# A scaled matmul on one core: the rows of two output tiles leave in transfers of 6, 5, 105 and 12 rows

## The chip, the cores and the metric

The kernel runs on one core of a Trainium2 chip. The core has a matrix engine (TensorE, PE in the profile), three engines for elementwise work (VectorE = DVE, ScalarE = ACT, GpSimd = POOL), an engine that here only issues transfers (SyncE = SP), and sixteen DMA engines that move data between the chip's memory (DRAM, "HBM" in the profile) and the on-chip memory of 128 partitions. The metric is the device time of one execution in microseconds (us), as a median over several runs.

## The reference

```python
"x": np.random.randn(16, 512, 1024).astype(np.float32)
"weight": np.random.randn(1024, 768).astype(np.float32)
"scale": np.float32(0.1)
"add_value": np.random.randn(16, 512, 768).astype(np.float32)

return (scale * np.matmul(x, weight) + add_value).astype(np.float32)
```

Seen as matrices, `x` is 8192 x 1024, `add_value` and the output are 8192 x 768. Every element of the three is moved once, and the weight once.

## The kernel before

The 8192 rows are 64 tiles of 128 rows, one row to a partition. They form three blocks of 24, 24 and 16 tiles. Within a block of g tiles, partition p holds g neighbouring rows of the matrix, so that several neighbouring tiles of a partition are one stretch of bytes in DRAM: a tile's row of output is 3 KB, and twelve neighbouring tiles are one run of 36 KB in each partition.

The buffers are rings: `xs` has 16 slots for tiles of `x`, `ao` has 32 slots for tiles of `add_value`, in which the output is also made (tile t is in slot (t + 8) mod 32, and the weight uses the first eight slots at the start).

What each engine does, in the order of one tile's way:
- **SyncE** (`sync_engine`) issues every transfer, in the order of the string `STREAM`, and waits ahead of each until its slots are free or its results made. A word such as `x16+8` loads tiles 16 to 23 of `x`, `a` loads `add_value`, `w` the weight, and `o32+16` stores the output tiles 32 to 47. All are 128 rows. The stores take turns on four semaphores (`o_sem`); a store also waits for the one that used its semaphore four stores earlier.
- **ScalarE and GpSimd** (`mover`) share the cast of `x` to bf16: a move is four tiles, and each engine casts half of the pieces, eight instructions for each move, into one of two buffers `va`. A move waits for the load (`x_sem`) and for the buffer to be free (`turned`). The first four moves are written out, the other twelve are in a loop of three turns.
- **VectorE** (`vector_engine`) transposes two tiles at a time from `va` into `xt` (`turn`, line 190; it waits for both movers), and finishes two tiles at a time (`finish`, line 199): product x scale + add_value, from `mm` into `ao`. Each finish adds 2 to the semaphore `made`, which starts at `MADE`.
- **TensorE** (`tensor_engine`, lines 222 and 248) multiplies the tiles in order, eight pieces of the contraction for each, in two parts of 512 and 256 columns.

The last store (`o62+2`) is issued behind the section with the hand-written order. The other stores of the second half are `o32+16`, `o48+8` and `o56+6`. The order of the transfers on SyncE is written out by hand; so are all waits.

The change touches `transfer` (line 97), `sync_engine` (line 107) and `mover` (line 151).

Of the kernel before, what the change touches and what calls it, by code (L numbers as in the profile page):

```python
# [7 lines left out]
P = 128  # L8
BLOCKS = ((0, 24), (24, 24), (48, 16))
G = 8  # L10
X_SLOTS = 16
# [5 lines left out]
MOVE = 4  # L17
O_LANES = 4
HALVED = (0, 1)
FETCH = 128  # L20

STREAM = """
    x0+4 w0+8 x4+8 a0+8 x12+4 a8+8 x16+8 a16+8 x24+8 a24+8 x32+8 o0+8 o8+8 a32+8 x40+8
    a40+8 x48+8 x56+4 o16+8 o24+8 a48+4 x60+4 a52+4 a56+8 o32+16 o48+8 o56+6 o62+2
"""


# [7 lines left out]
def kernel(  # L35
# [17 lines left out]
    T = M // P  # L53
# [4 lines left out]
    def blocks(flat):  # L58
        return [(s, g, flat[P * s:P * (s + g), :].rearrange("(p t) n -> p t n", t=g))
                for s, g in BLOCKS]  # L60

    x_v, add_v, out_v = blocks(x_f), blocks(add_f), blocks(out_f)
    w_v = weight.rearrange("(p r) n -> p r n", p=P)

    def rows(view, s, n):
        for first, g, block in view:
            if first <= s and s + n <= first + g:
                return block[:, s - first:s - first + n, :]
        raise ValueError((s, n))
# [5 lines left out]
    ao = const.tile([P, A_SLOTS, N], fp32, name="ao")  # L75
# [10 lines left out]
    by_act, by_pool, pool_go, turned, casts, done, made = (  # L86
        tc.alloc_semaphore(name)
        for name in ("by_act", "by_pool", "pool_go", "turned", "casts", "done", "made"))
    TURNED = MOVE * VA_BUFS
    MADE = TURNED + MM_BUFS  # L90

    def slots(t, n):
        k = (t + G) % A_SLOTS
        assert k + n <= A_SLOTS
        return slice(k, k + n)

    def transfer(eng, op, s, n):
        if op == "w":
            return eng.dma_start(ao[:, s:s + n, :], w_v[:, s:s + n, :])  # L99
        if op == "x":  # L100
            k = s % X_SLOTS
            return eng.dma_start(xs[:, k:k + n, :], rows(x_v, s, n))  # L102
        if op == "a":
            return eng.dma_start(ao[:, slots(s, n), :], rows(add_v, s, n))
        return eng.dma_start(rows(out_v, s, n), ao[:, slots(s, n), :])

    def sync_engine(eng):
        loads, stores, known = [], [], {}

        def need(sem, value):  # L110
            if known.get(id(sem), 0) < value:
                eng.wait_ge(sem, value)
                known[id(sem)] = value

        for op, s, n in stream[:-1]:
            last = s + n
            if op == "w":
                sem = w_sem
            elif op == "x":
                lane = s % X_SLOTS // MOVE  # L120
                if last > X_SLOTS:
                    moved = 8 * (last - X_SLOTS) // MOVE
                    need(by_act, moved)
                    need(by_pool, moved)
                if n == 2 * MOVE:
                    eng.sem_inc(x_sem[lane + 1], 16)
                sem = x_sem[lane]
            elif op == "a":
                if loads:
                    need(a_sem, 16 * len(loads))  # L130
                if slots(s, n).start < KJ:
                    need(casts, KJ)
                if s >= A_SLOTS:
                    for i, (a, b) in enumerate(stores):
                        if a < last - A_SLOTS and s - A_SLOTS < a + b:
                            need(o_sem[i % O_LANES], 16 * (i // O_LANES + 1))
                if s % G:
                    sem = a_late
                else:
                    sem = a_sem  # L140
                    loads.append((s, n))
            else:
                i = len(stores)
                if i >= O_LANES:
                    need(o_sem[i % O_LANES], 16 * (i // O_LANES))
                need(made, MADE + last)
                sem = o_sem[i % O_LANES]
                stores.append((s, n))
            transfer(eng, op, s, n).then_inc(sem, 16)

    def mover(eng, copy, parity, count, go=None):
        if go is None:
            eng.preload_act_table(mybir.ActivationFunctionType.Copy)  # L153

        def move(q, step, landed, freed):
            eng.wait_ge(x_sem[q], landed)
            if freed is not None:
                eng.wait_ge(turned, freed)
            if go is not None:
                eng.sem_inc(go, 1)  # L160
            k = MOVE * q
            src = xs[:, k:k + MOVE, :].rearrange("p i (b k) -> p i b k", b=4)
            for t in range(0, MOVE, step):
                for a in (parity, parity + 2):
                    for b in range(4):
                        copied = copy(va[q % VA_BUFS][32 * b:32 * b + 32, t:t + step, a, :],  # L166
                                      src[32 * a:32 * a + 32, t:t + step, b, :])
                        if step == MOVE or b % 2:
                            copied.then_inc(count, 1)

        for q in range(X_SLOTS // MOVE):
            move(q, MOVE // 2 if q in HALVED else MOVE, 16,
                 MOVE * (q + 1) if q >= VA_BUFS else None)
        with eng.Fori(32, T + 1, X_SLOTS) as i:
            for q in range(X_SLOTS // MOVE):
                move(q, MOVE, i, i + (4 * q - 12) if q < 3 else i)

    def vector_engine(eng):
        ao_g = ao.rearrange("p (g t) n -> p g t n", t=G)
# [73 lines left out]
    for eng in (nc.scalar, nc.gpsimd):  # L253
        eng.addr_align(FETCH, offset=0, max_nops=0)
    with tc.tile_critical(no_gpsimd_drain=True):  # L255
        sync_engine(nc.sync)
        mover(nc.scalar, nc.scalar.copy, 0, by_act)
        mover(nc.gpsimd, nc.gpsimd.tensor_copy, 1, by_pool, pool_go)
        vector_engine(nc.vector)
        tensor_engine(nc.tensor)  # L260
    transfer(nc.sync, *stream[-1])


# [33 lines left out]
```

## Time and profile before

| | |
|---|---|
| median of 3 runs | 209.46 us (209.31 to 209.88) |
| the profiled execution | 209.42 us |
| its span, first to last instruction | 207.6 us |
| bytes read from and written to DRAM | 61.87 MB and 25.17 MB |
| mean rate over the span | 419 GB/s |
| TensorE busy | 82% |
| GpSimd busy | 67% |
| ScalarE busy | 66% |
| VectorE busy | 59% |
| packets of SyncE's queue, share of 16 DMA engines' span | 98.0% |

The page of the profile gives busy times, the span in 40 slices, the DMA queues, the chain of work that ended last, groups of instructions and the transfers' times from issue to landing. Other views of the same execution list the instructions in order of time, who waited for whom, and busy times in chosen windows. A transfer issued is not a transfer done: SyncE's issue instruction is short, and the data move later. A packet in the DMA rows is one run of bytes or one write that reports completion.

### The profile page before, as it was taken

The numbers are of one execution on the slowest core, as the hardware profiler recorded it, in microseconds if no ns is written. First come the engines' busy times: TensorE is split into PE (matmuls) and PEld (weight loads), VectorE is DVE, ScalarE is ACT, GpSimd is POOL, SyncE is SP. The second block draws the span as 40 slices with busy tenths as digits, with TensorE's granted clock in tenths as the row PEclk, the third lists the DMA queues.
The fourth block names the chain that finished last, engine by engine and source line by source line (L and its number), as shares of the span: only waits on it lengthen the run. The fifth ranks groups of instructions, "written<-read, shape, count | busy, mean of one in ns | idle before, by whom it ended". The sixth has DMA issues, their size and how long they took to land.

```text
span 207.6 us, 2250 instructions
## 1 busy us (share of the span) xinstructions
PE 170.7 (82%) x1024; PEld 50.8 (24%) x512; DVE 123.0 (59%) x66; ACT 137.8 (66%) x145; POOL 138.3 (67%) x148
## 2 busy tenths in 40 slices
PE   0001993699999999999999999999999899999800
PEld 0000230123223333333333333333333233333200
DVE  0038304937677767776777677767774867777320
ACT  2494199999596969696969079999696959100000
POOL 0399299999797969696969179999796959200000
PEclk9999999699999999999999999999999999999995
DMA  6999999999999999899999999999999999998994
GB/s 224 458 432 410 448 455 404 455 455 404 404 473 436 420 388 505 350 421 440 436 431 447 404 450 459 404 420 436 436 421 428 412 455 469 455 445 355 434 420 173
DMA packets 4034, 87.05 MB, mean 419 GB/s; under 512 B 448, under 2 KB 448, under 8 KB 576
## 3 DMA queue, kind: packets, MB, share of 16 engines
q1 hardware_dynamic: 4032, 87.03, 98.0%
q14 instruction: 2, 0.02, 0.0%
HBM read 61.87 MB, written 25.17 MB: 419 GB/s over the span
## 4 chain that ended last, share of the span: by engine, by line
PE 59%; DMA 26%; POOL 5%; DVE 4%; issue 2%; SPq 0%; DVEq 0%; POOLq 0%
PE mm L248 39%; PE mm L222 20%; DMA xs<-in_x_dram 11%; DMA out_dram<-ao 10%; DMA ao<-in_add_value_dram 5%; POOL va L166 5%; DVE xt L190 2%; DVE ao L199 2%; SPq L99 0%; SPq L102 0%; DVEq L199 0%; DVEq L196 0%; POOLq L160 0%; DVEq L188 0%; SPq L292 0%
## 5 line engine op out<-in xcount | busy, mean ns | idle before, releaser
L248 PE MATMUL mm<-w_bf,xt 128*128 128x512 bf16 x512 | 170.3, 385 | 26.0 <-DVE w_bf L183 20.2
L166 POOL CAST va<-xs 32x1024 bf16<-32x1024 f32 (+1 forms) x144 | 138.1, 959 | 39.1 <-DMA xs<-in_x_dram 18.6
L166 ACT CAST va<-xs 32x1024 bf16<-32x1024 f32 (+1 forms) x144 | 136.5, 948 | 38.4 <-DMA xs<-in_x_dram 20.5
L222 PE MATMUL mm<-w_bf,xt 128*128 128x256 bf16 x512 | 141.4, 276 | 0.0
L199 DVE SCALAR_TENSOR_TENSOR ao<-mm,ao 128x1536 f32 (+1 forms) x32 | 56.2, 1755 | 58.7 <-PE mm L222 46.2
L248 PEld LDWEIGHTS mm<-w_bf,xt 128*128 128x128 bf16 x512 | 50.8, 99 | 145.4 <-issue 138.4
L190 DVE STREAM_TRANSPOSE xt<-va 128x1024 f32<-128x1024 f32 x32 | 65.2, 2037 | 16.9 <-POOL va L166 16.9
L183 DVE CAST w_bf<-ao 128x3072 bf16<-128x3072 f32 x2 | 4.3, 2170 | 0.0
L153 ACT ACT_TABLE_LOAD x1 | 1.3, 1283 | 1.3 <-SPq L255 1.3
L278 POOL MEMSET const-float32-0.0<- 128x1 f32 x1 | 0.1, 98 | 0.2 <-issue 0.2
L278 POOL MEMSET const-bfloat16-1.0<- 128x1 bf16 x1 | 0.1, 100 | 0.0
L278 POOL MEMSET const-uint8-127<- 128x1 uint8 x1 | 0.1, 98 | 0.0
L278 POOL MEMSET const-float32-1.0<- 128x1 f32 x1 | 0.1, 97 | 0.0
## 6 DMA issues: line engine op xcount, KB each, us to landing
xs<-in_x_dram SPq DMA_DIRECT2D x6, 4096.0 KB, 20.5
ao<-in_add_value_dram SPq DMA_DIRECT2D x7, 3072.0 KB, 17.0
out_dram<-ao SPq DMA_DIRECT2D x5, 3072.0 KB, 22.4
xs<-in_x_dram SPq DMA_DIRECT2D x4, 2048.0 KB, 14.3
out_dram<-ao SPq DMA_DIRECT2D x1, 6144.0 KB, 29.9
ao<-in_weight_dram SPq DMA_DIRECT2D x1, 3072.0 KB, 14.0
ao<-in_add_value_dram SPq DMA_DIRECT2D x2, 1536.0 KB, 9.9
out_dram<-ao SPq DMA_DIRECT2D x1, 2304.0 KB, 11.5
```

The costliest lines, as they stand in the source:

```text
L153: eng.preload_act_table(mybir.ActivationFunctionType.Copy)
L166: copied = copy(va[q % VA_BUFS][32 * b:32 * b + 32, t:t + step, a, :], src[32 * a:32 * a + 32, t:t + step, b, :])
L183: eng.tensor_copy(w_bf[:, s:s + n, :], ao[:, s:s + n, :]).then_inc(casts, n)
L190: eng.transpose(xt[:, 2 * half:2 * half + 2, :, :].rearrange("p i c (a m) -> p i c a m", a=4), pairs.rearrange("p i a (k c) -> p i c a k", ...
L199: eng.scalar_tensor_tensor(a, mm[:, q:q + 2, 0:N], float(scale), a, op0=mybir.AluOpType.mult, op1=mybir.AluOpType.add).then_inc(made, 2)
L222: return eng.add_instruction(mybir.InstMatmult(name=nc.get_next_instruction_name(), engine=eng.engine, ins=[eng.lower_ap(weights), eng.low ...
L248: eng.matmul(mm[:, q, 0:CUT], piece, w_bf[:, j, 0:CUT], **flags)
L278: nc = _bacc.Bacc("TRN2", target_bir_lowering=False, num_devices=1)
```

## The change

The store of tiles 32 to 47 becomes a store of tiles 32 to 43. Of the four tiles left, 44 and 46 go in one store of their own from SyncE (the new word `e44+4`: every second tile of four, all 128 rows, two runs of 3 KB a row). Tiles 45 and 47 are cut by rows: SyncE stores rows 0 to 5, and GpSimd stores rows 6 to 10, 11 to 115 and 116 to 127, each with two runs of 3 KB a row and a semaphore of its own.

GpSimd issues its three transfers ahead of its last move (tiles 60 to 63), behind a wait until tile 47 is finished. To make this place, the loop of both movers is cut at other points: three moves are written out, then come three turns of four moves, then the last move. ScalarE waits at its end until the four row transfers have landed.

```diff
+SPREAD = (44, 4)
+SPREAD_ROWS = (("SP", 6), ("Pool", 5), ("Pool", 105), ("Pool", 12))
...
-    a40+8 x48+8 x56+4 o16+8 o24+8 a48+4 x60+4 a52+4 a56+8 o32+16 o48+8 o56+6 o62+2
+    a40+8 x48+8 x56+4 o16+8 o24+8 a48+4 x60+4 a52+4 a56+8 o32+12 e44+4 o48+8 o56+6 o62+2
...
+        if op == "e":
+            return eng.dma_start(rows(out_v, s, n)[:, 0::2, :], ao[:, slots(s, n), :][:, 0::2, :])
...
+    spread_sem = [tc.alloc_semaphore(f"spread{i}") for i in range(len(SPREAD_ROWS))]
+
+    def spread(eng, name):
+        first = 0
+        for (by, n), sem in zip(SPREAD_ROWS, spread_sem):
+            if by == name:
+                eng.dma_start(rows(out_v, *SPREAD)[first:first + n, 1::2, :],
+                              ao[first:first + n, slots(*SPREAD), :][:, 1::2, :]).then_inc(sem, 16)
+            first += n
+        assert first == P
...
             transfer(eng, op, s, n).then_inc(sem, 16)
+            if op == "e":
+                spread(eng, "SP")
...
-        for q in range(X_SLOTS // MOVE):
+        for q in range(3):
             move(q, MOVE // 2 if q in HALVED else MOVE, 16,
                  MOVE * (q + 1) if q >= VA_BUFS else None)
-        with eng.Fori(32, T + 1, X_SLOTS) as i:
-            for q in range(X_SLOTS // MOVE):
-                move(q, MOVE, i, i + (4 * q - 12) if q < 3 else i)
+        with eng.Fori(16, T, X_SLOTS) as i:
+            move(3, MOVE, i, i)
+            for q in range(3):
+                move(q, MOVE, i + 16, i + 4 * (q + 1))
+        if go is not None:
+            eng.wait_ge(made, MADE + sum(SPREAD))
+            spread(eng, "Pool")
+        move(3, MOVE, T, T)
+        if go is None:
+            for sem in spread_sem:
+                eng.wait_ge(sem, 16)
```

## The prediction

> **What bounds the kernel now.** I read the page first: engines' busy shares, the DMA row of the slices, the queue, then the chain.
>
> ```profile
> span 207.6 us, 2250 instructions
> PE 170.7 (82%) x1024; PEld 50.8 (24%) x512; DVE 123.0 (59%) x66; ACT 137.8 (66%) x145; POOL 138.3 (67%) x148
> DMA  6999999999999999899999999999999999998994
> q1 hardware_dynamic: 4032, 87.03, 98.0%
> PE 59%; DMA 26%; POOL 5%; DVE 4%; issue 2%; SPq 0%; DVEq 0%; POOLq 0%
> ```
>
> The chain gives TensorE 59%, but the queue row says otherwise: the packets of SyncE's queue fill 98.0% of sixteen DMA engines' span. The chain steps from the last store back to what allowed its issue, and so back into the matmuls; it doesn't see that the store was issued into a full queue. The issue rows show that:
>
> ```profile
> out_dram<-ao SPq DMA_DIRECT2D x1, 6144.0 KB, 29.9
> out_dram<-ao SPq DMA_DIRECT2D x1, 2304.0 KB, 11.5
> out_dram<-ao SPq DMA_DIRECT2D x1, 768.0 KB, 7.9
> ```
>
> The 768 KB store of tiles 62 and 63 takes 7.9 us to land, though at the 430 GB/s of the row 191 to 197 below 0.786 MB take 1.8 us. Most of the rest is time behind other transfers. So the DMA engines set the end, and what counts is when the last of the sixteen is done. The windows over the tail show it; the columns after PEclk are the mean share of the 16 engines and GB/s. Shares over 1 show that a run's whole time is booked where it starts.
>
> ```profile
> core 0: us, PE busy (x) PEld busy (x) DVE busy (x) ACT busy (x) POOL busy (x), PEclk, DMA share, GB/s
> 191.00:197.00 6.00, 5.70 (x36) 1.57 (x16) 1.96 (x2) 0.00 (x0) 0.00 (x0) 1.00 1.00 430
> 203.20:204.20 1.00, 0.00 (x0) 0.00 (x0) 0.00 (x0) 0.00 (x0) 0.00 (x0) 0.50 1.01 424
> ...
> 204.40:204.80 0.40, 0.00 (x0) 0.00 (x0) 0.00 (x0) 0.00 (x0) 0.00 (x0) 0.50 0.52 215
> 204.80:205.20 0.40, 0.00 (x0) 0.00 (x0) 0.00 (x0) 0.00 (x0) 0.00 (x0) 0.50 0.19 77
> 205.20:205.60 0.40, 0.00 (x0) 0.00 (x0) 0.00 (x0) 0.00 (x0) 0.00 (x0) 0.50 0.07 31
> 205.60:206.00 0.40, 0.00 (x0) 0.00 (x0) 0.00 (x0) 0.00 (x0) 0.00 (x0) 0.50 0.04 15
> 206.00:206.30 0.30, 0.00 (x0) 0.00 (x0) 0.00 (x0) 0.00 (x0) 0.00 (x0) 0.50 0.05 20
> 206.30:207.60 1.30, 0.00 (x0) 0.00 (x0) 0.00 (x0) 0.00 (x0) 0.00 (x0) 0.50 0.00 0
> ```
>
> One engine is 1/16 = 0.06. The three windows from 205.20 to 206.30 hold 0.07x16x0.40 + 0.04x16x0.40 + 0.05x16x0.30 = 0.95 us of work: one engine, alone, for four rows of the last store. A 6 KB row takes 6144 / (424/1.01/16 = 26.2 bytes per ns) = 234 ns, and the last starts after 206.00, so I put this engine's end at 206.25. The others start nothing after 205.2; I put the latest of them there. The windows from 204.40 on hold 3.3 + 1.2 + 0.95 = 5.5 us, 0.34 us an engine; with half a row carried in, an even share would end near 204.85. **One engine is about 1.4 us behind the mean and 1.05 us behind the next.** Before the change each transfer has 128 rows, eight for each engine, so this is not a count of bytes; this engine is slower at the same work.
>
> **The change, part by part.**
>
> *Shorter runs.* Between long and short rows the windows give the price of a run. The window 191 to 197 (mostly rows of 24 KB, tiles 48 to 55) has 430/16 = 26.9 bytes per ns, so 914 ns a row; 6 KB cost 234 ns. The difference of 680 ns for 18,432 bytes leaves 234 - 227 = 7 ns for a run as such. 3 KB runs aren't shown; by this line one takes 121 ns and a row of two 241 ns. Before, a row of tiles 32 to 47 is one run of 48 KB; after it is one of 36 KB, two of 3 KB in the store of 44 and 46, and two of 3 KB in the spread transfers: four runs more, x 8 rows x 7 ns = 0.23 us an engine. Five more transfers end instead of one longer one; at one such 7 ns for a completion that is 0.04 us. **Every engine gains 0.27 us of work.** This holds for GpSimd's queue as well only if its runs cost what SyncE's do, which no row shows: its queue isn't used before. Lower bound of the difference: 0 (the bytes and engines are the same); upper bound: another 121 ns a run, a doubling. I take 0, being nearest to the only store rows there are, and keep the upper end for a rival.
>
> *Uneven shares.* Tiles 45 and 47 are 128 rows of 6 KB, eight an engine before. Row counts of 6, 5, 105 and 12 can't be dealt evenly to sixteen. My assumption, which no row shows: a transfer goes in whole equal shares over as many engines as its count allows, so 105 = 15 x 7 leaves one engine out, and 5, 12 and 6 give one row each to as many engines. The left-out engine then has between 0 and 3 of its 8 rows, so 1.2 to 1.9 us less work (5 to 8 x 241 ns), and the five to eight rows go to others, one each (0.24 us) if well placed. Bounds for the engine that is late: from -1.9 to +0.48 us (two rows extra). I take -5 rows for it and +1 for five others: the four counts sum to 128 in just this way if the two small GpSimd transfers together go once round without the sixteenth share.
>
> [...]
>
> *Sum.* Late engine: 206.25 + 0.27 - 5 x 0.241 = 205.31. Latest of the others: 205.2 + 0.27 = 205.47, or 205.71 if it gets a row. The end moves from 206.25 to 205.47 or 205.71, midpoint 205.59: -0.66 us. The profiled execution took 209.42 us (1.8 around its span), the median of the runs is 209.46, so 209.42 - 0.66 = **208.8 us**.
>
> *What is hidden.* SyncE issues two transfers more and a 12-tile store after tile 43 instead of a 16-tile store after 47.
>
> ```profile
> 161.23 0.80 SPq L104 DMA_DIRECT2D ao<-in_add_value_dram  x2
> 162.08 37.10 SPq L105 DMA_DIRECT2D out_dram<-ao  x4
> ...
> SPq L105 <- DVE ao L199: 30.5, 2, 15.3
> ...
> SPq L292 <- DMA out_dram<-ao: 7.5, 1, 7.5
> ```
>
> Two issues took 0.80 us, so two more cost 0.8; the next store, of tiles 48 to 55, waits for VectorE, two waits of this kind being 30.5 us, so they disappear there. Only beyond about 15 us would they show. The extra store also shifts which earlier store's landing each later one waits for, but those landed long before (29.9 us was the longest). The earlier issue of the 12 tiles gains nothing: at 162.08 all its tiles are finished anyway, and the queue is full. SyncE's last wait, 7.5 us at the end, is the landing of the last store.
>
> GpSimd waits until tile 47 is finished, then issues three transfers, then casts its share of tiles 60 to 63; queued behind the wait are only these, and VectorE and so TensorE need them.
>
> ```profile
> 154.34 1.76 DVE L199 SCALAR_TENSOR_TENSOR ao<-mm,ao 128x1536 f32 x1 [1.48 <-PE mm L222]
> ...
> 170.84 1.76 DVE L199 SCALAR_TENSOR_TENSOR ao<-mm,ao 128x1536 f32 x1 [2.00 <-PE mm L222]
> ...
> 181.23 1.76 DVE L199 SCALAR_TENSOR_TENSOR ao<-mm,ao 128x1536 f32<-128x1536 f32 x1 [1.49 <-PE mm L222]
> 182.91 2.00 DVE L190 STREAM_TRANSPOSE xt<-va 128x1024 f32<-128x1024 f32 x1
> ...
> 196.80 1.76 DVE L199 SCALAR_TENSOR_TENSOR ao<-mm,ao 128x1536 f32<-128x1536 f32 x1 [3.44 <-PE mm L222]
> ```
>
> ```profile
> 158.21 8.70 POOL L166 CAST va<-xs 32x1024 bf16<-32x1024 f32 x8 [1.68 <-DVE xt L190]
> 169.00 8.70 POOL L166 CAST va<-xs 32x1024 bf16<-32x1024 f32 x8 [2.10 <-DVE xt L190]
> ...
> L166 POOL CAST va<-xs x144: 599/1033/2042, 8.2 to 176.7; 32x1024 bf16<-32x1024 f32 x112, 32x512 bf16<-32x512 f32 x32
> ```
>
> Counted back from the last, the finish at 154.34 is tiles 46 and 47, done at 156.1; GpSimd is busy to 166.9, so the wait costs nothing. Its next casts start at 169.0 (2.1 us free), end at 177.7, and are turned at 182.91: 5.2 us more, 7.3 together. What GpSimd takes to issue a transfer isn't shown: SyncE's 0.4 us is the near bound, its own longest instruction, 2.04 us, the far one. Three make 1.2 to 6.1 us; both fit. If the cover is gone, each us over 7.3 delays the last stores, which have some us of their own in the 7.9. ACT's wait at its end falls due long before the end.
>
> GpSimd's transfers start near 168 in a queue of their own and so pass SyncE's queued loads: 122 x 241 ns / 16 = 1.8 us of all engines. The add-tiles for the finishes at 170.84 and 181.23 are ahead of them. Those finishes waited 2.00 and 1.49 us for TensorE, not for a load; a finish late by 1.8 us would be made good by the last store's wait in the queue.
>
> The casts' loops are cut elsewhere: 3 + 3 x 4 + 1 moves instead of 4 + 3 x 4, sixteen either way, in the same order. The backward branch now falls between other moves; these waits of 1.7 to 2.1 us cover it.
>
> **The rivals.**
> *The late engine is not the one spared (209.7 to 209.9).* It keeps eight rows, or gets a ninth: 206.25 + 0.27, or + 0.51, so 209.69 or 209.93. For it: nothing in the trace ties the late engine to a row number. Against: the counts leave just about the surplus (5 rows, 1.2 us) that this engine shows (1.4 us). It decides if the late engine is spared fewer than two rows.
> [...]
> *GpSimd's runs are dearer (210.1 to 210.6, the slower side).* 244 runs are 15.25 an engine. At double the price each engine gains 15.25 x 121 ns = 1.85 us: 208.76 + 1.85 = 210.6. Break-even is 0.66/15.25 = 43 ns a run, and 0.3% slower begins at 85 ns. For it: no row has this queue. Against: a run as such costs 7 ns on SyncE's queue, a sixth of that.
> *GpSimd's issues hold up the last tiles.* That needs over 2.4 us an issue (7.3/3) and then more than the queue's slack; above the far bound of 2.04. At 4 us an issue it would be 4.7 us late, of which I'd expect 1 to 2 at the end, 210.4 to 211.4.
> *Another dealing (209.1).* If the shares always start at the first engine, five engines get two rows extra and one gets none: 205.2 + 0.27 + 0.48 = 205.95, so 209.1.
>
> **How the numbers follow.** 0.3% of 209.46 is 0.63 us, about what a measurement of this kernel can tell from no change: faster is under 208.83, slower over 210.09. Forecast: 0.50 (own range 208.4 to 208.95, of it 0.40 faster, 0.10 within). Late engine not spared: 0.20 (0.12 within, 0.08 slower, with somewhat dearer runs on top). Dearer runs: 0.20, slower. Other dealing: 0.08, within. Held-up tiles: 0.02, slower. So 0.40, 0.30, 0.30. The range goes from 208.4 up to 210.3, which leaves out the worse half of the dearer runs, the held-up tiles and a rest below.
>
> **What would show it.** Right: a second queue with 244 data runs; in the tail's windows no stretch of about 1 us with a share of 0.06 or less, but all engines ending within about 0.5 us, near 205.6. Wrong: that lone stretch is still there and ends near 206.5 (not spared); the queue's time a packet is well over 121 ns (dearer); GpSimd's last casts start after 171 and the finish that ends at 198.56 (196.80 + 1.76) moves with them (held up). It would be wrong most simply if the engine that is late in this execution is not late in most.

## The result, and the profile after

| | before | after |
|---|---|---|
| median | 209.46 us (209.31 to 209.88) | 208.63 us (208.52 to 208.82) |
| the profiled execution | 209.42 us | 208.55 us |
| its span | 207.6 us | 206.8 us |

The ratio is 0.9957, with a 95% interval of 0.9943 to 0.9972: 0.6 to 1.2 us faster. The forecast was 208.8 in a range of 208.4 to 210.3.

The page of the kernel after, in the order in which it was read before (span, DMA row of the slices, queues, chain), and the costs and issues that are new:

```profile
span 206.8 us, 2264 instructions
DMA  6999999999999899999999999999999999999996
q1 hardware_dynamic: 4322, 86.28, 97.6%
q0 software_dynamic: 192, 0.75, 0.9%
PE 77%; DMA 11%; POOL 5%; DVE 2%; issue 1%; SPq 0%; DVEq 0%; POOLq 0%
L117 POOL DMA_DIRECT2D out_dram<-ao x3 | 2.0, 659 | 0.0
...
out_dram<-ao POOLq DMA_DIRECT2D x1, 630.0 KB, 16.2
out_dram<-ao POOLq DMA_DIRECT2D x1, 72.0 KB, 18.4
out_dram<-ao POOLq DMA_DIRECT2D x1, 30.0 KB, 6.6
```

The last digit of the DMA row goes from 4 to 6: a larger part of the last slice is work of all engines, in a shorter span. The chain again names TensorE, now with 77%, and is again no guide, since TensorE didn't become the limit. GpSimd's queue, q0, is new. The windows over the tail of the kernel after (columns as in the prediction; the last two are the mean share of the sixteen DMA engines and GB/s):

```profile
204.40:204.80 0.40, 0.00 (x0) 0.00 (x0) 0.00 (x0) 0.00 (x0) 0.00 (x0) 0.50 0.95 399
204.80:205.20 0.40, 0.00 (x0) 0.00 (x0) 0.00 (x0) 0.00 (x0) 0.00 (x0) 0.50 0.30 123
205.20:205.60 0.40, 0.00 (x0) 0.00 (x0) 0.00 (x0) 0.00 (x0) 0.00 (x0) 0.50 0.01 0
205.60:206.00 0.40, 0.00 (x0) 0.00 (x0) 0.00 (x0) 0.00 (x0) 0.00 (x0) 0.50 0.00 0
```

Before, the window from 204.40 had a share of 0.52 and one engine worked alone until about 206.25. After, that window is at 0.95, and no data run starts after 205.20 (0 GB/s), so with 234 ns for the last 6 KB row everything has ended by 205.43. The lone stretch is gone, and with it about 0.8 us, which is the gain. The kept traces also hold the start and duration of each packet, which no view lists; by the sixteen last completions of the last store, fifteen engines end between 204.4 and 205.16 before and one at 206.25, while all sixteen end between 204.6 and 205.35 after. The five runs after lie between 208.52 and 208.82, so by their times the spared engine was the late one in each of them, not only in the profiled one.

### The profile page after: what moved, and what is told of

Same layout as the page of the kernel before. It is cut to its first block, busy times and chain, and to the rows that moved or that the text cites. A ratio compares the mean times of both kernels' runs of the same rounds, so it can differ in the third digit from the quotient of the medians.

```text
span 206.8 us, 2264 instructions
## 1 busy us (share of the span) xinstructions
PE 170.9 (83%) x1024; PEld 50.8 (25%) x512; DVE 122.8 (59%) x66; ACT 137.8 (67%) x145; POOL 140.4 (68%) x151
## 3 DMA queue, kind: packets, MB, share of 16 engines
q1 hardware_dynamic: 4322, 86.28, 97.6%
## 4 chain that ended last, share of the span: by engine, by line
PE 77%; DMA 11%; POOL 5%; DVE 2%; issue 1%; SPq 0%; DVEq 0%; POOLq 0%
PE mm L273 51%; PE mm L247 26%; DMA xs<-in_x_dram 11%; POOL va L183 5%; DVE xt L215 1%; DVE ao L224 1%; SPq L101 0%; SPq L104 0%; POOLq L177 0%; DVEq L213 0%; SPq L317 0%; DVEq L221 0%; SPq L141 0%; SPq L280 0%
## 5 line engine op out<-in xcount | busy, mean ns | idle before, releaser
L208 DVE CAST w_bf<-ao 128x3072 bf16<-128x3072 f32 x2 | 3.8, 1944 | 0.0
L117 POOL DMA_DIRECT2D out_dram<-ao x3 | 2.0, 659 | 0.0
```

Source lines behind the costliest of these rows:

```text
L117: eng.dma_start(rows(out_v, *SPREAD)[first:first + n, 1::2, :], ao[first:first + n, slots(*SPREAD), :][:, 1::2, :]).then_inc(sem, 16)
L208: eng.tensor_copy(w_bf[:, s:s + n, :], ao[:, s:s + n, :]).then_inc(casts, n)
```

## The experiments

Each kernel below is the kernel after with the edit shown, unless it says otherwise. "Before" is the kernel before, run on the same chip beside it.

| kernel | median | ratio to before, 95% interval |
|---|---|---|
| 45 and 47 whole, from SyncE | 209.63 | 1.0012 (1.0003 to 1.0021) |
| 45 and 47 whole, from GpSimd | 209.55 | 1.0005 (0.9996 to 1.0014) |
| counts 9, 105, 8 from GpSimd | 209.82 | 1.0017 (1.0008 to 1.0026) |
| the loops of the casts alone | 209.46 | 0.9998 (0.9989 to 1.0007) |
| neighbours 46 and 47 | 210.0 | 1.0029 (1.0018 to 1.004) |
| half of the columns | 209.25 | 0.9989 (0.998 to 0.9998) |
| four tiles | 211.67 | 1.0095 (1.0079 to 1.011) |
| four tiles, SyncE's store later | 211.07 | 1.0086 (1.0071 to 1.0101) |
| short runs of SyncE first | 209.09 | 0.9984 (0.9975 to 0.9993) |
| four tiles, whole, from GpSimd | 209.56 | 1.0007 (0.9998 to 1.0016) |

The first four separate three theories: *Placing* (the forecast: the late DMA engine gets five rows less), *Queue* (a second queue fed by GpSimd gains by itself) and *Splitting* (the cut of the store or of the loops gains).

**Tiles 45 and 47 whole, from SyncE.**

```diff
-SPREAD_ROWS = (("SP", 6), ("Pool", 5), ("Pool", 105), ("Pool", 12))
+SPREAD_ROWS = (("SP", 128),)
```

> Tiles 45 and 47 leave in one transfer of 128 rows from SyncE; all else as after the change. Placing (the gain is the late DMA engine's five rows): the sixteen engines have eight rows each again, so the lone stretch of about 1 us at the end is back, and four runs of 3 KB a row more than before cost 8 x 4 x 7 ns = 0.23 us: 209.6 to 209.8. Queue (a second queue fed by GpSimd gains, whichever rows it has): no gain either, 209.6 to 209.8. Splitting (the gain comes from the cut of the 16-tile store or of the casts' loops): as after the change, 208.6.

Measured: 209.63 us. Its windows over the tail:

```profile
205.20:205.60 0.40, 0.00 (x0) 0.00 (x0) 0.00 (x0) 0.00 (x0) 0.00 (x0) 0.50 0.11 46
205.60:206.00 0.40, 0.00 (x0) 0.00 (x0) 0.00 (x0) 0.00 (x0) 0.00 (x0) 0.50 0.07 31
206.00:206.40 0.40, 0.00 (x0) 0.00 (x0) 0.00 (x0) 0.00 (x0) 0.00 (x0) 0.50 0.04 15
```

The lone engine (0.04 to 0.07) is back, with a row that starts after 206.00. Same bytes, same short runs, equal shares: the whole gain is lost and the short runs' price is left, 0.06 to 0.44 us by the interval against 0.23 expected. Splitting in its first form falls.

**Tiles 45 and 47 whole, from GpSimd.**

```diff
-SPREAD_ROWS = (("SP", 6), ("Pool", 5), ("Pool", 105), ("Pool", 12))
+SPREAD_ROWS = (("Pool", 128),)
```

> Tiles 45 and 47 leave in one transfer of 128 rows from GpSimd; all else as after the change. Placing: equal shares again, the late engine ends alone near 206.4, and with GpSimd's 6 KB rows at the 234 ns of SyncE's the runs cost a little less than in the kernel above: 209.5 to 209.7. Queue: 208.6, as after the change. Splitting: 208.6.

Measured: 209.55 us. Two lines of its DMA view and one of its tail:

```profile
q1 hardware_dynamic: 4304, 86.25, 97.2%
q0 software_dynamic: 144, 0.79, 0.9%
...
206.00:206.40 0.40, 0.00 (x0) 0.00 (x0) 0.00 (x0) 0.00 (x0) 0.00 (x0) 0.50 0.04 15
```

Even more bytes than with the change go through GpSimd's queue (0.79 MB against 0.75), and nothing is gained; the lone engine is still at work after 206. Queue falls: a second issuing engine with equal shares left the time as it was before (1.0005). The change gains by unequal shares, not by a second queue.

The queue row also shows SyncE's side of the dealing. The kernel after has 4322 packets there, this one 4304. The 18 more are the 6-row transfer: 12 data runs and 6 completions, so it ran on six engines.

**Another engine spared.**

```diff
-SPREAD_ROWS = (("SP", 6), ("Pool", 5), ("Pool", 105), ("Pool", 12))
+SPREAD_ROWS = (("SP", 6), ("Pool", 9), ("Pool", 105), ("Pool", 8))
```

> As after the change, but GpSimd's counts are 9, 105, 8 in place of 5, 105, 12 (SyncE's 6 as they were). If shares are dealt round from where the last transfer stopped, another engine is spared (six rows) and the one spared after the change has nine. Placing: the late engine ends alone near 206.25 + 0.2 + 0.24 = 206.7, 209.8 to 209.9 (209.6 if it has eight). Queue: 208.6. Splitting: 208.6. If the dealing doesn't depend on the count of the first transfer, also 208.6.

Measured: 209.82 us. Its tail:

```profile
205.20:205.60 0.40, 0.00 (x0) 0.00 (x0) 0.00 (x0) 0.00 (x0) 0.00 (x0) 0.50 0.08 31
205.60:206.00 0.40, 0.00 (x0) 0.00 (x0) 0.00 (x0) 0.00 (x0) 0.00 (x0) 0.50 0.07 31
206.00:206.40 0.40, 0.00 (x0) 0.00 (x0) 0.00 (x0) 0.00 (x0) 0.00 (x0) 0.50 0.07 31
206.40:206.80 0.40, 0.00 (x0) 0.00 (x0) 0.00 (x0) 0.00 (x0) 0.00 (x0) 0.50 0.00 0
```

The same number of uneven transfers, the same queues, the same bytes: slower than before, with an engine that is alone for over a microsecond, and two rows of it (0.07 x 16 x 0.40 = 0.45 us) after 206.00. Only which engine is spared has changed. This is the run that shows Placing.

The packet records show the shares themselves. A packet starts some 3 ns before the end of the one ahead of it on its engine, so in time order the packets fall into sixteen strings. This is worked out from the starts and durations, stands in no view, and is ambiguous at single places. In the kernel after, fifteen strings hold eight of GpSimd's rows and one holds two, and six strings, that one among them, also hold a row of SyncE's: 3, 9 and 8 rows an engine, as the prediction assumed. The string with three rows ends near 205.3. With 9, 105, 8 one string again holds two of GpSimd's rows and ends at 203.6, and the late one, which ends at 206.6, holds eight and one of SyncE's, so nine.

Since only the first and the last count differ, this run also shows that the engine left out by the 105 rows depends on the count before them: with 5 rows ahead it is the late engine, which then has three rows and ends near 205.3, with 9 rows ahead it is another, and the late one has nine rows and ends at 206.6. How the place follows from the count these two runs don't show.

**The loops of the casts alone.** No row transfers and one store of tiles 32 to 47, so the kernel before with the new loops.

```diff
-SPREAD_ROWS = (("SP", 6), ("Pool", 5), ("Pool", 105), ("Pool", 12))
+SPREAD_ROWS = ()
...
-    a40+8 x48+8 x56+4 o16+8 o24+8 a48+4 x60+4 a52+4 a56+8 o32+12 e44+4 o48+8 o56+6 o62+2
+    a40+8 x48+8 x56+4 o16+8 o24+8 a48+4 x60+4 a52+4 a56+8 o32+16 o48+8 o56+6 o62+2
...
-        if go is not None:
-            eng.wait_ge(made, MADE + sum(SPREAD))
-            spread(eng, "Pool")
```

> The kernel before with the casts' loops of after (three moves, three turns of four, one move); stores as before, GpSimd issues nothing. Placing and Queue: 209.4 to 209.5, as before. Splitting, in its form that the loops gain: under 209.2.

Measured: 209.46 us, ratio 0.9998 (0.9989 to 1.0007). No effect of the loops can be seen.

**Neighbours, runs joined.**

```diff
-SPREAD = (44, 4)
+SPREAD = (46, 2)
...
-    a40+8 x48+8 x56+4 o16+8 o24+8 a48+4 x60+4 a52+4 a56+8 o32+12 e44+4 o48+8 o56+6 o62+2
+    a40+8 x48+8 x56+4 o16+8 o24+8 a48+4 x60+4 a52+4 a56+8 o32+14 o48+8 o56+6 o62+2
...
-                eng.dma_start(rows(out_v, *SPREAD)[first:first + n, 1::2, :],
-                              ao[first:first + n, slots(*SPREAD), :][:, 1::2, :]).then_inc(sem, 16)
+                eng.dma_start(rows(out_v, *SPREAD)[first:first + n, :, :],
+                              ao[first:first + n, slots(*SPREAD), :]).then_inc(sem, 16)
...
-            if op == "e":
+            if (op, s) == ("o", 32):
+                eng.wait_ge(made, MADE + sum(SPREAD))
                 spread(eng, "SP")
```

> The same row counts (6 SyncE; 5, 105, 12 GpSimd), but of the neighbouring tiles 46 and 47, one run of 6 KB a row; SyncE stores tiles 32 to 45 in one transfer of 42 KB rows. If the dealing goes by the row counts alone: the same engine is spared, and two runs a row of SyncE's fewer than after the change (8 x 2 x 7 ns = 0.11 us): 208.4 to 208.6. If runs that join are dealt another way, always from the first engine on (rows 10, 10, 10, 10, 10, 9, 8 x 6, 7, 7, 7, 0): the late engine, which the run with 9, 105, 8 puts among the first six, gets ten rows: 206.25 + 0.1 + 0.48 = 206.8, or 209.9 to 210.1.

Measured: 210.0 us. Its DMA view and tail:

```profile
q0 software_dynamic: 192, 0.75, 0.9%
...
205.20:205.60 0.40, 0.00 (x0) 0.00 (x0) 0.00 (x0) 0.00 (x0) 0.00 (x0) 0.50 0.19 77
205.60:206.00 0.40, 0.00 (x0) 0.00 (x0) 0.00 (x0) 0.00 (x0) 0.00 (x0) 0.50 0.08 31
206.00:206.40 0.40, 0.00 (x0) 0.00 (x0) 0.00 (x0) 0.00 (x0) 0.00 (x0) 0.50 0.07 31
```

The same row counts and bytes, with fewer short runs, are 1.4 us slower than the change: the late engine isn't spared, and several others are later too (0.19 at 205.2 to 205.6, three engines' worth, where the kernel with 9, 105, 8 has 0.08). The prediction's "other dealing", five engines with ten rows and one with none, gives this time if the late engine is among those that get more. The strings of packets bear the dealing out: one engine has none of GpSimd's rows and is done at 203.9, three have seven rows, and the other twelve fit the ten, nine and eight rows of the expectation; whether the late engine has nine or ten they don't settle. Rows of one joined run are thus dealt otherwise than rows of two runs. So two separate runs a row, which is what tiles that aren't neighbours give, are part of what makes the change work.

**Half the columns.**

```diff
+HALF = 384
...
-                eng.dma_start(rows(out_v, *SPREAD)[first:first + n, 1::2, :],
-                              ao[first:first + n, slots(*SPREAD), :][:, 1::2, :]).then_inc(sem, 16)
+                eng.dma_start(rows(out_v, *SPREAD)[first:first + n, 1::2, 0:HALF],
+                              ao[first:first + n, slots(*SPREAD), 0:HALF][:, 1::2, :]).then_inc(sem, 16)
...
+                eng.dma_start(rows(out_v, s, n)[:, 1::2, HALF:], ao[:, slots(s, n), HALF:][:, 1::2, :]).then_inc(half_sem, 16)
...
```

> As after the change, but only columns 0 to 383 of tiles 45 and 47 go in the four row transfers; the other half goes in one transfer of 128 rows from SyncE (two runs of 1.5 KB a row). Placing: the five rows spared are half as long, 5 x 121 = 0.6 us, and 16 more runs cost 0.11 us: with tiles 45 and 47 whole and 128 rows from SyncE it was 209.63, so 209.63 + 0.1 - 0.6 = 209.1 (209.0 to 209.3), and a lone stretch of about 0.4 us is left at the end. If what counts were only that some engine is spared: 208.6.

Measured: 209.25 us. Its tail:

```profile
205.20:205.60 0.40, 0.00 (x0) 0.00 (x0) 0.00 (x0) 0.00 (x0) 0.00 (x0) 0.50 0.15 61
205.60:206.00 0.40, 0.00 (x0) 0.00 (x0) 0.00 (x0) 0.00 (x0) 0.00 (x0) 0.50 0.04 15
206.00:206.40 0.40, 0.00 (x0) 0.00 (x0) 0.00 (x0) 0.00 (x0) 0.00 (x0) 0.50 0.00 0
```

Half the bytes spared give 209.63 - 209.25 = 0.4 us of the 1.0 between whole transfers and the change, and a lone stretch half as long is left. The forecast had 0.5 here, with 209.25 inside its range. The gain goes by how much this engine is relieved.

**Four tiles.**

```diff
-SPREAD = (44, 4)
+SPREAD = (40, 8)
...
-    a40+8 x48+8 x56+4 o16+8 o24+8 a48+4 x60+4 a52+4 a56+8 o32+12 e44+4 o48+8 o56+6 o62+2
+    a40+8 x48+8 x56+4 o16+8 o24+8 a48+4 x60+4 a52+4 a56+8 o32+8 e40+8 o48+8 o56+6 o62+2
```

> As after the change, but the row transfers carry four tiles (41, 43, 45, 47, four runs of 3 KB a row), and 40, 42, 44, 46 go in SyncE's own store. Placing: the late engine is spared 2.4 us, more than its surplus, and is now idle early; the five that get a row more end 0.48 us later and set the end: 205.2 + 0.2 + 0.2 + 0.48 = 206.0 to 206.1, so 209.2 to 209.3; no engine ends alone. If more rows spared were simply better: 207.8 or below.

Measured: 211.67 us, a miss by over 2 us. The windows and the queue of its profiled execution (213.37 us, the slowest of five; span 211.6):

```profile
180.00:185.00 5.00, 5.00 (x32) 1.47 (x15) 3.51 (x3) 0.00 (x0) 0.00 (x0) 1.00 1.01 418
185.00:190.00 5.00, 5.00 (x33) 1.56 (x16) 3.51 (x3) 0.00 (x0) 0.00 (x0) 1.00 0.94 291
...
q0 software_dynamic: 336, 1.50, 2.2%
```

Engines are taken for 0.94 of the time from 185 to 190 but move 291 GB/s. GpSimd's queue holds 2.2% of 16 x 211.6 us = 74 us for 244 packets of 6 KB (two for each of 122 rows), about 300 ns each, where the 6 KB rows of the last store cost 234. Three runs look for the reason.

**Four tiles, SyncE's short-run store later; and, with two tiles, that store earlier.**

```diff
-SPREAD = (44, 4)
+SPREAD = (40, 8)
...
-    a40+8 x48+8 x56+4 o16+8 o24+8 a48+4 x60+4 a52+4 a56+8 o32+12 e44+4 o48+8 o56+6 o62+2
+    a40+8 x48+8 x56+4 o16+8 o24+8 a48+4 x60+4 a52+4 a56+8 o32+8 o48+8 e40+8 o56+6 o62+2
```

> The kernel with doubled rows missed its forecast (211.67 instead of 209.2 to 209.3). Its rate fell to 291 GB/s at 185 to 190 us, while GpSimd's rows were still under way beside SyncE's 3 KB runs of tiles 40 to 46. Here that store comes behind the store of tiles 48 to 55, after GpSimd's rows have landed; the same bytes in the same shares. Overlap (GpSimd's rows and SyncE's short runs slow each other): the rest of the forecast holds, 209.2 to 209.6. Amount (twice the bytes through GpSimd's queue cost this much wherever they go): 211 or more.

```diff
-    a40+8 x48+8 x56+4 o16+8 o24+8 a48+4 x60+4 a52+4 a56+8 o32+12 e44+4 o48+8 o56+6 o62+2
+    a40+8 x48+8 x56+4 o16+8 o24+8 a48+4 x60+4 a52+4 a56+8 e44+4 o32+12 o48+8 o56+6 o62+2
```

> As after the change, but SyncE's short-run store of tiles 44 and 46 (and its 6 rows) goes ahead of the store of tiles 32 to 43, into the time of GpSimd's rows. Overlap: GpSimd's packets take clearly more than the 234 to 241 ns a row, its share rises above 0.9%, and the time is 208.8 to 209.6. Amount: 208.6, as after the change, since all bytes and shares are the same.

Measured: 211.07 and 209.09 us. The queue rows, of the first and of the second, and the landing of the second's largest GpSimd transfer:

```profile
q0 software_dynamic: 336, 1.50, 2.2%
```

```profile
q0 software_dynamic: 192, 0.75, 1.0%
...
out_dram<-ao POOLq DMA_DIRECT2D x1, 630.0 KB, 10.3
```

With four tiles, moving the short runs away leaves the price as it was (2.2%). So overlap isn't what made the four tiles dear, and its forecast for this run (209.2 to 209.6) falls. With two tiles, putting the short runs beside GpSimd's rows costs 0.46 us against the change (the intervals 0.9975 to 0.9993 and 0.9943 to 0.9972 lie apart), and GpSimd's share rises from 0.9% to 1.0%. Both are as Overlap forecast (208.8 to 209.6), but that Overlap is the cause isn't shown. By the packet records 74 of GpSimd's 122 rows start while SyncE's 3 KB runs are under way, and 69 of them take the plain price of 234 ns or at most 11 ns more. Five, all between 177.7 and 178.1 us, take 374 to 1196 ns, and they make nearly all of the rise (258 ns in the mean instead of 241); after the change, without short runs beside them, three rows take 315 to 605. What makes the 0.46 us stays open.

**Four tiles, whole, from GpSimd.**

```diff
-SPREAD = (44, 4)
-SPREAD_ROWS = (("SP", 6), ("Pool", 5), ("Pool", 105), ("Pool", 12))
+SPREAD = (40, 8)
+SPREAD_ROWS = (("Pool", 128),)
...
-    a40+8 x48+8 x56+4 o16+8 o24+8 a48+4 x60+4 a52+4 a56+8 o32+12 e44+4 o48+8 o56+6 o62+2
+    a40+8 x48+8 x56+4 o16+8 o24+8 a48+4 x60+4 a52+4 a56+8 o32+8 e40+8 o48+8 o56+6 o62+2
```

> Tiles 41, 43, 45, 47 in one transfer of 128 rows from GpSimd (eight rows an engine), 40, 42, 44, 46 in SyncE's own store, in the order of the kernel with doubled rows (211.67). There, and with SyncE's store put later (211.07), GpSimd's 244 packets took 2.2% of sixteen engines' span, about 300 ns each, where 234 is the price of 6 KB. Amount (so many bytes in GpSimd's queue are dear as such): again about 300 ns a packet, and 211 or more. Uneven dealing (rows read by other engines than those that read them in a 128-row transfer are dear, once there are many): 234 to 240 ns a packet (256 packets, 1.8% of the span); no engine is spared, 40 short runs an engine more than before cost 0.3 us less GpSimd's joined ones: 209.6 to 209.9.

Measured: 209.56 us. Its queue:

```profile
q0 software_dynamic: 272, 1.57, 1.8%
```

1.8% of 16 x 207.6 us is 60 us for 256 packets, 234 ns each: the plain price. So the amount in GpSimd's queue costs nothing by itself. Four tiles are dear only when cut by rows; this run takes away the uneven shares and the cut into several transfers together, so it doesn't say which of the two it is. The packet records show what dear means: single rows that take far longer, not all rows a little longer. Of GpSimd's packets 46 of 244 take over 26 ns more than the plain price of their length with four tiles cut by rows (the longest takes 1775 ns), 3 of 122 after the change, none of 92 with half of the columns, and none of the 256 here. Why this becomes dear at four tiles and hardly at two stays open.

## Why the prediction was right, point by point

**The bound.** Right. The sixteen full DMA engines (98.0% of their span) and the last of them set the end: relieving it moved the time, and TensorE's last product is no earlier after the change. The finish of the last tiles starts at 197.02 instead of 196.80, and the kernel still ends sooner.

```profile
197.02 1.76 DVE L224 SCALAR_TENSOR_TENSOR ao<-mm,ao 128x1536 f32<-128x1536 f32 x1 [3.44 <-PE mm L247]
```

**Shorter runs, 0.27 us an engine.** Right. By the queue rows the packets' time is 98.0% of 207.6 = 203.45 us an engine before and (97.6 + 0.9)% of 206.8 = 203.70 after: 0.25 more, as far as rows with one decimal tell. The packet records give 203.57 and 203.78, 0.21 more, and 121 ns for SyncE's runs of 3 KB, the price that the line between the windows gave.

**GpSimd's rows at SyncE's price.** Right in price, wrong in form. I expected 244 data runs; its queue has 192 packets, of which 122 are of 6 KB and 70 of 8 bytes or less, and with four tiles whole, 272 packets for 256 pairs of 3 KB runs and 16 completions. So two runs go as one packet of 6 KB, at 234 ns where I had 241; that a packet is one run of bytes holds for SyncE's queue alone. At 0.9% the whole queue costs 30 us for 122 rows, about 244 ns each with the small packets among them. The rival with dearer runs (85 ns more a run) was wrong for this change; at four tiles a milder form of it did appear, in some rows only.

**Uneven shares.** Right, and it was the assumption that carried everything. The shares are those that the strings of packets show: three rows for one engine, nine for five, eight for ten. That the spared engine is the late one was in part luck: no row of before tied the late engine to a row number, and the only argument was that the counts fit its surplus. The runs with 9, 105, 8 and with neighbours show how narrow it was: the first of them is the rival "late engine not spared" (209.69 to 209.93 forecast, 209.82 measured), the second the rival "other dealing", for which I had given 209.1 and which came out at 210.0. The step that failed there: I let the engine without rows be the late one. It is one of those that get nine or ten.

**The sum.** The sign and mechanism were right, the size a little low: -0.66 forecast, -0.87 between the two profiled executions. The term that was mis-sized is the end of the latest of the others. I put it at 205.47 or, with a row more, 205.71; the windows after put the end at 205.43 or earlier, and the packet records at 205.35. The five engines that got a row more end between 204.7 and 205.1, so they were not the latest ones before. The late engine itself, forecast to end at 205.31, ends near 205.3.

**What is hidden.** SyncE's and GpSimd's rows after:

```profile
162.60 0.43 SPq L108 DMA_DIRECT2D out_dram<-ao  x1
163.07 0.41 SPq L117 DMA_DIRECT2D out_dram<-ao  x1
...
SPq L109 <- DVE ao L224: 29.7, 2, 15.2
```

```profile
159.32 8.70 POOL L183 CAST va<-xs 32x1024 bf16<-32x1024 f32 x8 [1.71 <-DVE xt L215]
167.97 1.97 POOL L117 DMA_DIRECT2D out_dram<-ao  x3
169.99 8.69 POOL L183 CAST va<-xs 32x1024 bf16<-32x1024 f32 x8
```

SyncE's two issues cost 0.84 us (0.8 forecast), and its wait for VectorE shrinks by just that, from 30.5 to 29.7. GpSimd's three take 1.97 us, within the bounds of 1.2 to 6.1, and its next casts start about 1 us later than before, inside the 5.2 us of cover. Both were right.

One point here was wrong without a price. I had GpSimd's rows pass SyncE's queue in a block of 1.8 us. They land 6.6 to 18.4 us after issue: in the strings of packets, rows of GpSimd and of SyncE mostly alternate one by one, so a 6 KB row of GpSimd (234 ns) waits behind a row of SyncE of 24 or 36 KB (912 or 1364 ns). The landing of 10.3 us instead of 16.2, where some of SyncE's runs beside them were of 3 KB (121 ns), fits it.

## What to carry to other kernels

When DMA engines are full to the end, look at the last microseconds in narrow windows: here a share of 0.04 to 0.07 of sixteen engines that lasted about 1 us was one engine alone, and then its bytes counted, not the mean rate. The lag was evened out with transfers of 6, 5, 105 and 12 rows (0.83 us gained), but only where they spared that engine: the same trick aimed elsewhere cost 0.36 us. Check how rows are dealt with a run that moves the spared place, and measure a larger amount before using it, since four tiles instead of two turned the gain into a loss of 2 us.

## What was not expected of the hardware

- Rows that form one joined run were dealt to the engines in another way than rows of two runs, with equal row counts: 210.0 against 208.63 us.
- Unevenly dealt rows from GpSimd cost about the plain price with two tiles (244 ns with all small packets) but about 300 ns with four, while four tiles in one transfer of 128 rows cost 234.
- In every kernel here with equal shares one DMA engine is alone at the end, up to about 1 us after the next (206.25 against 205.16 us before), also where only SyncE issues. What makes it late wasn't tried.
